# One of four weight sums moved to DRAM, and three more seven-product groups, in a hybrid decoder layer

## The chip, the cores and the metric

One core of a Trainium2 chip runs the whole layer in one launch. The metric is device microseconds of one execution. Engines are named as in the profile: PE is TensorE (PEld its weight loads), DVE is VectorE, ACT is ScalarE, POOL is GpSimd, SP is SyncE; a name with a q (SPq, ACTq) is that engine's queue, which also issues DMAs.

## What is computed

A decoder layer of width 2048 on 256 tokens, float32 throughout:

```python
u = rmsnorm(h, norm_mix_pre)
z, xbc, dt, q, k, v = split(u @ w_in)            # w_in: 2048 x 14368 columns in six parts
y_ssm = ssd(conv_silu(xbc), dt) gated by silu(z) # Mamba-2 scan, 32 heads in 8 groups
y_att = dilated_window_attention(q, k, v)        # 16 heads
h = h + rmsnorm(concat(y_ssm, y_att) @ w_out, norm_mix_post)   # w_out: 4096 x 2048
f = relu(rmsnorm(h, norm_mlp_pre) @ w_up) ** 2                 # w_up: 2048 x 8192
h = h + rmsnorm(f @ w_down, norm_mlp_post)                     # w_down: 8192 x 2048
```

## The kernel before, in words

The weights are 287 MB of traffic and each is used once, on 256 tokens, so the kernel streams weights past activations that stay in SBUF. To reach float32 accuracy, every operand is split into a high part (`hi`, rounded by ACT in `split`, L139) and a remainder (`lo`, subtracted by DVE, L140), and each product becomes three matmuls: high by high, high by low, low by high.

A weight step takes two rows of 128 (KB = 2, one index `k` stands for the pair) by 512 columns (NB): `fetch` loads them as one 512 KB DMA on SP's queue into a tile `raw` (four of them, and in some stages two more in a region called `uc`), and the split fills a pair of tiles `hi` and `lo` (five pairs, BUFS). In the first part (up to about 400 us: SSD projections, queries and keys) features come out on partitions (`gemm_features`, L393 and L396). From the values on, tokens come out on partitions, and a `unit` works on two column blocks at once, for both token tiles.

For each `k` a unit has the choice of two forms. The ordinary one (`row_tiles`, L262 to L264) multiplies two token tiles, two rows and two column blocks directly: 8 products, 24 matmuls. The other one (`seven`, L344 to L346) is a Winograd scheme with seven products, 21 matmuls. For it DVE makes sums of the weights (L225, through `add_in_line`), all of 128x512: with a0, a1 the two rows of the first column block and b0, b1 those of the second, these are a0 + b0, then that + b1, then that + a1, and b0 + b1 in place. The four splits of a seven are those of `raw_a`, of the two-row tile of sums `e`, of `raw_b`, and of one row `t4`. It also needs sums of the activations, made once for a `k` by `sums_of_acts` (L302 to L305 and a split), which a later unit on the same activations uses again. After a unit's last seven, `combine` folds four extra PSUM banks (`more`) into the result. The lists of `k` in each unit, and which of them go by seven, are written out by hand: `V_SEVENS` for the two units of values, `UP_SEVENS` for the seven units of w_up, and literal tuples for two units of w_out, two of the first half of w_down and two of the second. There are 59 sevens. The first unit of w_out begins with `k = 5`; the first five are done before it, between steps of the attention heads.

The order on each engine comes from a scheduler that takes what is ready, by priority, the place in the program being the default priority. Weight work runs in `tc.high_priority(offset=AHEAD)`, that is ahead of all ordinary work. `in_line` keeps the splits and sums of one engine in written order. `tc.issue_after(x)` is the tool for ordering one instruction behind `x`; `attention` (PE behind PE) and `copies` (a DMA of ACT behind an ACT split or, where there is none, behind the last matmul, `product[1]`) use it. Other work is written as generators in a deque, and `pump` runs a step of one of them after each weight step.

POOL does little: zeros at the edge of the convolution (L655), some elementwise steps of the SSD groups (L701, L703, L723), and the powers that make reciprocal roots (L134, L885, L1160). It issues no DMA. `rsqrt_mean` makes `rstd` there, early in the kernel; from it `over_partitions` makes `rbc`, by which the convolutions scale their inputs.

Of the kernel before, what the change touches and what calls it, by code (L numbers as in the profile page):

```python
# [10 lines left out]
F32 = mybir.dt.float32  # L11
# [3 lines left out]
ALU = mybir.AluOpType  # L15

P = 128
# [20 lines left out]
COL_V = COL_K + NH * DH  # L38
NB = 512
KB = 2  # L40
MASKED = -1.0e30
PAIRS = ((128, 1), (512, 4), (2048, 16))
AHEAD = 1_000_000
# [7 lines left out]
FIRST = 3  # L51
UP_SEVENS = (2, 4, 5)
V_SEVENS = (1, 3, 5, 6)


def constants():
# [18 lines left out]
def hymba_layer(ctx: ExitStack, tc: tile.TileContext, x, norm_mix_pre, w_in, conv_w, conv_b, dt_bias, a_log,  # L75
                d_skip, ssm_norm_w, w_out, norm_mix_post, norm_mlp_pre, w_up, w_down, norm_mlp_post,
                consts, out):
    nc = tc.nc
    w_in, w_out, w_up, w_down = w_in[0], w_out[0], w_up[0], w_down[0]
# [61 lines left out]
        return (nc.scalar.activation(hi, src, AF.Copy, scale=scale),  # L141
                nc.vector.scalar_tensor_tensor(lo, src, scale, hi.bitcast(F32), op0=ALU.mult, op1=ALU.subtract))

    def fetch(src, k0, c0, step=KB, into=None):

        raw = wp.tile([P, KB, NB], F32, name="raw", bufs=RAWS) if into is None else into
        for j in range(0, KB, step):
            rs = slice((k0 + j) * P, (k0 + j + step) * P)
            nc.sync.dma_start(raw[:, j:j + step], src[rs, c0:c0 + NB].rearrange("(k p) n -> p k n", p=P))
        return raw  # L150
# [13 lines left out]
    room = {}  # L164
# [22 lines left out]
        room["acts"] = acts  # L187
        sums_of.clear()

    def fetch_next(src, k0, c0):  # L190

        if room["raw"] is None:
            return fetch(src, k0, c0)
        turn = room["turn"]
        room["turn"] += 1
        n = KB * (turn % (RAWS + (NK - SUMS) // KB - 1) - RAWS)
        return fetch(src, k0, c0, into=None if turn < 0 or n < 0 else room["raw"][:, n:n + KB])

    def parts():
        return [wp.tile([P, KB, NB], F32R, name=n, bufs=BUFS) for n in ("hi", "lo")]  # L200
# [2 lines left out]
    product = {}  # L203
# [5 lines left out]
    line = {}  # L209
# [10 lines left out]
        with in_line():  # L220
            line["act"], line["dve"] = split(hi, lo, raw)

    def add_in_line(dst, a, b):
        with in_line():
            line["dve"] = nc.vector.tensor_tensor(dst, a, b, op=ALU.add)  # L225

    def weights(src, k0, c0, fetch=fetch):

# [82 lines left out]
    def seven(src, ca, cb, k, acc, more, first, last):  # L311


        ch, cl = sums_of_acts(k)
        h_, l_, r = room["acts"](k * KB)
        with tc.high_priority(offset=AHEAD):
            raw_a = fetch_next(src, k * KB, ca)
            raw_b = fetch_next(src, k * KB, cb)
            e, t4 = sum_tile(), tmp()
            add_in_line(e[:, 0], raw_a[:, 0], raw_b[:, 0])  # L320
            add_in_line(e[:, 1], e[:, 0], raw_b[:, 1])
            hl_a = parts()
# [12 lines left out]

        def summed(i):
            return ch[:, i], cl[:, i]

        for dst, (a_h, a_l), (hi, lo), j, own in (
                (more[0], block(0, 0), hl_a, 0, True), (acc[0], block(1, 0), hl_a, 1, False),  # L340
                (more[1], summed(1), hl_e, 0, True), (more[2], summed(2), hl_e, 1, True),
                (more[3], summed(0), hl_b, 0, True), (acc[1], summed(3), hl_b, 1, False),
                (acc[2], block(1, 1), hl_t, 0, False)):
            nc.tensor.matmul(dst, a_h, hi[:, j], start=own and first, stop=False)  # L344
            nc.tensor.matmul(dst, a_h, lo[:, j], start=False, stop=False)  # L345
            nc.tensor.matmul(dst, a_l, hi[:, j], start=False, stop=own and last)  # L346
# [12 lines left out]
    def order_of(ks, by_seven):  # L359
        return [(k, k in by_seven) for k in ks]  # L360
# [445 lines left out]
    def keys_too(hb):  # L806
        return queries(COL_Q + hb * NB, rbq), queries(COL_K + hb * NB, rbc)
# [11 lines left out]
    def two_values(vb):  # L819

        if vb:
            room["own"] = deque(mp.tile([P, NT, NB], F32, name="tk", bufs=3)[:, t] for t in range(NT))
        room["sum"] = mp.tile([P, 4, S], F32, name="cT", bufs=5).rearrange("p (k f) s -> p k (f s)", k=KB)
        values = [mp.tile([P, NT, NB], F32, name="tk", bufs=3) for _ in range(2)]
        more = [psmall(), bank(), psmall(), bank()]
        acc = [bank() for _ in range(2 * NT)]

        def end(b):
            def at_end(t, a):
                with tc.high_priority(offset=AHEAD):  # L830
# [5 lines left out]
        unit(w_in[:, COL_V:], vb, order_of(range(7), V_SEVENS), (7,), acc, more,  # L836
             lambda x: combine_new([[v[:, t] for t in range(NT)] for v in values], x), 0, (end(0), end(1)))
        return values

# [236 lines left out]

    in_place_of_u()
    acc = [bank() for _ in range(2 * NT)]
    early = 5
    for k in range(early):  # L1080
# [31 lines left out]
    def whole(n):  # L1112
        def at_end(t, a):
# [18 lines left out]
    def first_hidden(t, acc):  # L1132
# [11 lines left out]
    unit(w_out, 2, order_of((0, 6, 1, 9, 2, 12, 3, 4, 5, 8, 7, 10), (6, 9, 12, 4, 8, 10)), (11, 13, 14, 15), acc, more,  # L1144
         lambda x: combine_new(in_mw(2), x), ending=mix_to_up)
    begun = ended.pop()
    over_partitions(rbc, rmlp)
# [88 lines left out]
    for hf in range(2):  # L1236
        if hf:
            in_place_of_h(act_u)
        for fb in range(0 if hf else 2, 8, 2):
            unit(w_up[:, hf * 4096:], fb, order_of(range(6), UP_SEVENS), (6, 7), acc, more,  # L1240
                 lambda x: combine_new(room["shared"], x), 0, (up_end(fb, 0), up_end(fb + 1, 1)))
            acc, more = more, acc
        if hf == 0:
            in_place_of_h(part)
            unit(w_down, 0, order_of(range(14), (4, 6, 9, 11, 13)), (14, 15), acc, more,
                 lambda x: combine_new(in_mw(0), x), 0, (onto(0), onto(1)))
            unit(w_down, 2, order_of((0, 1, 4, 2, 6, 3, 9, 5, 11, 7, 13, 8), (4, 6, 9, 11, 13)), (10, 12, 14, 15), more, acc,
                 lambda x: combine_new(in_mw(2), x), 0, (onto(2), onto(3)))
    new_h()

# [19 lines left out]
    unit(w_down[4096:], 2, order_of((0, 1, 3, 2, 6, 4, 8, 5, 11, 7, 13, 9), (3, 6, 8, 11, 13, 9)), (10, 12, 14, 15), more, acc,  # L1270
         lambda x: combine_onto(2, x), LAG_DOWN, (complete(2), finish))


# [21 lines left out]
```

## Time and profile before

| | us |
|---|---|
| median of 3 runs | 1473.88 |
| lowest and highest run | 1473.48 and 1474.70 |
| span of the profiled execution, first to last instruction | 1471.1 |
| around the span, by the median | 2.8 |

The profiled execution has no time of its own beside the three runs, so the distance from its span to their median is what stands for the launch around it. A row of the stage table gives a stretch in us, its length, then busy time and number of instructions of each engine, the granted TensorE clock as a share, the mean share of 16 DMA engines, and GB/s. A row of instruction groups gives line, engine, operation, output and inputs with shapes and count, then busy time, mean ns, and the idle time before them with what ended it. A row of waits gives who waited for whom: us in all, times, longest. A row of the timeline gives start and duration in us. A DMA row gives count, size and us from issue to landing.

### The profile page before, as it was taken

Reading aid. Unit: us, or ns where it says so; the run is one execution under the profiler, and the core shown is the slowest. Engines: PE = TensorE matmul, PEld = TensorE weight load, DVE = VectorE, ACT = ScalarE, POOL = GpSimd, SP = SyncE. Lnnn points to the kernel's source line nnn. Section 1 sums busy time; section 2 is a strip of 40 time slices with the busy share of each in tenths; the row PEclk is TensorE's granted clock in tenths of the full one; section 3 lists DMA queues with packets and bytes.
Section 4 is the critical chain, followed back from the end, with each engine's and each line's share of the span. In section 5 each row is a group of like instructions: output and inputs, shape, how many; then the busy total and the mean of one; then the engine's idle time right before and its main releaser. Section 6 shows DMA issues by size and latency. Waiting matters only on the chain.

```text
span 1471.1 us, 20006 instructions
## 1 busy us (share of the span) xinstructions
PE 1461.2 (99%) x7216; PEld 1231.4 (84%) x7216; DVE 1239.6 (84%) x1849; ACT 861.1 (59%) x1188; POOL 47.8 (3%) x67
## 2 busy tenths in 40 slices
PE   9999999999999999999999999999999999999998
PEld 8888888888888888888888888888888888888886
DVE  6798797898497696588989989889887898989998
ACT  7475675465456565555557566655554666665553
POOL 0003100210000000000000000000000000000000
PEclk9999999999999999999999999999999999999999
DMA  7665566555657476566657566655665666576853
GB/s 272 208 205 182 179 184 194 174 172 167 177 168 207 122 208 192 191 229 210 204 177 237 165 194 201 210 175 191 213 223 174 201 201 205 172 235 202 273 200 114
DMA packets 151299, 287.31 MB, mean 195 GB/s; under 512 B 11696, under 2 KB 14624, under 8 KB 151200
## 3 DMA queue, kind: packets, MB, share of 16 engines
q1 hardware_dynamic: 143472, 272.50, 58.9%
q10 hardware_dynamic: 7728, 13.54, 2.8%
q8 instruction: 56, 0.92, 0.3%
q14 instruction: 43, 0.35, 0.1%
HBM read 281.78 MB, written 4.23 MB: 194 GB/s over the span
## 4 chain that ended last, share of the span: by engine, by line
PE 94%; DVE 3%; issue 1%; ACT 1%; DMA 1%; POOL 0%; POOLq 0%; SPq 0%; ACTq 0%; DVEq 0%
PE acc L393 17%; PE acc L262 12%; PE acc L263 12%; PE acc L264 12%; PE acc L396 9%; PE acc L345 4%; PE acc L346 4%; PE acc L344 4%; PE ps L263 3%; PE ps L262 3%; PE ps L264 3%; PE ps L346 2%; PE ps L344 2%; PE ps L345 2%; DVE lo L140 1%
## 5 line engine op out<-in xcount | busy, mean ns | idle before, releaser
L139 ACT ACTIVATE hi<-raw 128x1024 fp32r<-128x1024 f32 (+1 forms) x477 | 499.0, 1053 | 387.9 <-PE acc L393 111.9
L140 DVE TENSOR_TENSOR lo<-raw,hi 128x1024 fp32r<-128x1024 f32 (+1 forms) x477 | 579.9, 1220 | 135.7 <-ACT hi L139 127.9
L393 PE MATMUL acc<-ua,hi 128*128 128x512 f32 x680 | 186.3, 402 | 0.0
L393 PEld LDWEIGHTS acc<-ua,hi 128*128 128x128 f32 x680 | 119.7, 189 | 18.7
L262 PE MATMUL acc<-hi,ua 128*128 128x512 f32 x280 | 112.0, 400 | 0.0
L396 PEld LDWEIGHTS acc<-ua,lo 128*128 128x128 f32 x680 | 99.8, 189 | 11.6
L264 PE MATMUL acc<-hi,ua 128*128 128x512 f32 x280 | 109.3, 391 | 0.0
L263 PE MATMUL acc<-lo,ua 128*128 128x512 f32 x280 | 109.3, 390 | 0.0
L396 PE MATMUL acc<-ua,lo 128*128 128x256 f32 x680 | 102.9, 281 | 0.0
L262 PE MATMUL acc<-hi,sh 128*128 128x512 f32 x224 | 88.7, 397 | 0.0
L264 PE MATMUL acc<-hi,sl 128*128 128x512 f32 x224 | 87.3, 390 | 0.0
L263 PE MATMUL acc<-lo,sh 128*128 128x512 f32 x224 | 87.3, 390 | 0.0
L139 ACT ACTIVATE hi<-e 128x1024 fp32r<-128x1024 f32 x51 | 54.1, 1062 | 55.5 <-DVE e L225 50.3
L393 PE MATMUL acc<-uc,hi 128*128 128x512 f32 x272 | 77.6, 398 | 0.0
L263 PE MATMUL acc<-lo,ah 128*128 128x512 f32 x168 | 65.5, 390 | 0.4 <-DVE lo L140 0.4
L264 PE MATMUL acc<-hi,al 128*128 128x512 f32 x168 | 65.4, 389 | 0.0
L262 PE MATMUL acc<-hi,ah 128*128 128x512 f32 x168 | 65.4, 389 | 0.0
L264 PEld LDWEIGHTS acc<-hi,ua 128*128 128x128 f32 x280 | 52.6, 188 | 11.6
L140 DVE TENSOR_TENSOR lo<-e,hi 128x1024 fp32r<-128x1024 f32 x51 | 62.0, 1216 | 0.0
L262 PEld LDWEIGHTS acc<-hi,ua 128*128 128x128 f32 x280 | 52.6, 188 | 10.4 <-ACT ua L141 0.3
L263 PEld LDWEIGHTS acc<-lo,ua 128*128 128x128 f32 x280 | 52.7, 188 | 10.0
L264 PE MATMUL acc<-hi,uc 128*128 128x512 f32 x144 | 56.0, 389 | 0.0
(475 smaller groups left out, 3060.9 us busy)
## 6 DMA issues: line engine op xcount, KB each, us to landing
raw<-in_w_in_dram SPq DMA_DIRECT2D x189, 512.0 KB, 3.6
raw<-in_w_up_dram SPq DMA_DIRECT2D x128, 512.0 KB, 3.9
raw<-in_w_down_dram SPq DMA_DIRECT2D x110, 512.0 KB, 4.7
raw<-in_w_out_dram SPq DMA_DIRECT2D x46, 512.0 KB, 4.2
uc<-in_w_out_dram SPq DMA_DIRECT2D x18, 512.0 KB, 4.5
uc<-in_w_down_dram SPq DMA_DIRECT2D x18, 512.0 KB, 5.1
bc<-acs_d ACTq DMA_DIRECT2D x8, 512.0 KB, 4.5
xs<-in_x_dram SPq DMA_DIRECT2D x8, 256.0 KB, 6.3
```

Source lines behind the costliest of these rows:

```text
L139: return (nc.scalar.activation(hi, src, AF.Copy), nc.vector.tensor_tensor(lo, src, hi.bitcast(F32), op=ALU.subtract))
L140: nc.vector.tensor_tensor(lo, src, hi.bitcast(F32), op=ALU.subtract))
L262: nc.tensor.matmul(dst, a_h[:, r, ts], hi[:, j], start=begin and j == 0, stop=False)
L263: nc.tensor.matmul(dst, a_h[:, r, ts], lo[:, j], start=False, stop=False)
L264: product[t] = nc.tensor.matmul(dst, a_l[:, r, ts], hi[:, j], start=False, stop=end and j == KB - 1)
L344: nc.tensor.matmul(dst, a_h, hi[:, j], start=own and first, stop=False)
L345: nc.tensor.matmul(dst, a_h, lo[:, j], start=False, stop=False)
L346: nc.tensor.matmul(dst, a_l, hi[:, j], start=False, stop=own and last)
L393: nc.tensor.matmul(acc[f], hi[:, j, f * P:(f + 1) * P], u(k0 + j), start=k0 + j == 0, stop=False, skip_group_check=True)
L396: nc.tensor.matmul(acc[f][:, 0], lo[:, j, f * P:(f + 1) * P], u(k0 + j)[:, 0], start=False, stop=k0 + j == NK - 1, skip_group_check=True)
```

## The change

Two things. First, the sum b0 + b1 is no longer made by DVE. For each seven, POOL's queue issues a copy of b0 (256 KB) from the weights to a fresh DRAM tile `pair<n>`, and then a second DMA that adds b1 to it; `fetch` then loads the row `raw_b[:, 0]` from that tile and `raw_b[:, 1]` from the weights, in two DMAs on SP's queue where it was one. DVE makes three sums instead of four: a0 + (b0 + b1), that - b1, and that + a1. `plan` lists all pairs in the order of use; `next_pair` starts one, and each seven starts the pair of four sevens later (`PAIRS_AHEAD`). The first four are started before the first unit of values.

Second, three more groups go by seven: k = 8 and 10 in w_out's first unit (its order becomes 5, 6, 7, 8, 11, 9, 13, 10, 12), and k = 9 in the first unit of w_down's second half (its order changes too). All three are sevens already in the unit after, on the same activations. There are 62 sevens.

```diff
+PAIRS_AHEAD = 4
...
-    def fetch(src, k0, c0, step=KB, into=None):
+    def fetch(src, k0, c0, step=KB, into=None, pair=None):
         raw = wp.tile([P, KB, NB], F32, name="raw", bufs=RAWS) if into is None else into
+        if pair is not None:
+            nc.sync.dma_start(raw[:, 0], pair)
+            nc.sync.dma_start(raw[:, 1], src[(k0 + 1) * P:(k0 + 2) * P, c0:c0 + NB])
+            return raw
...
+    def plan(name, src, n, order, by_seven):
+        orders[name, n] = order_of(order, by_seven)
+        pairs.extend((src, n * NB, k) for k in order if k in by_seven)
+
+    def next_pair():
+        if not pairs:
+            return
+        src, ca, k = pairs.pop(0)
+        cb = slice(ca + NB, ca + 2 * NB)
+        d = dram.tile([P, NB], F32, name=f"pair{len(paired)}")
+        with ExitStack() as order:
+            for t in product:
+                order.enter_context(tc.issue_after(product[t].ins))
+            nc.gpsimd.dma_start(d, src[k * KB * P:(k * KB + 1) * P, cb])
+        nc.gpsimd.dma_start(d, src[(k * KB + 1) * P:(k * KB + 2) * P, cb], accum_op=ALU.add)
+        paired.append((src, ca, k, d))
+
+    def pair_of(src, ca, k):
+        next_pair()
+        s_, c_, k_, d = paired[turn_of["pair"]]
+        turn_of["pair"] += 1
+        return d
...
             raw_a = fetch_next(src, k * KB, ca)
-            raw_b = fetch_next(src, k * KB, cb)
+            raw_b = fetch_next(src, k * KB, cb, pair_of(src, ca, k))
             e, t4 = sum_tile(), tmp()
-            add_in_line(e[:, 0], raw_a[:, 0], raw_b[:, 0])
-            add_in_line(e[:, 1], e[:, 0], raw_b[:, 1])
+            add_in_line(e[:, 1], raw_a[:, 0], raw_b[:, 0])
+            add_in_line(e[:, 0], e[:, 1], raw_b[:, 1], ALU.subtract)
             hl_a = parts()
             split_in_line(*hl_a, raw_a)
             add_in_line(t4, e[:, 1], raw_a[:, 1])
-            add_in_line(raw_b[:, 0], raw_b[:, 0], raw_b[:, 1])
...
+    plan("out", w_out, 0, (5, 6, 7, 8, 11, 9, 13, 10, 12), (6, 8, 9, 10, 12))
...
+    plan(("down", 1), w_downs[1], 0, (0, 1, 2, 3, 4, 6, 5, 8, 7, 9, 10, 11, 12, 13), (3, 6, 8, 9, 11, 13))
...
     waiting.append(in_place_of_last_heads())
+    for _ in range(PAIRS_AHEAD):
+        next_pair()
     qk.append(keys_too(1))
...
-    unit(w_out, 0, order_of(range(early, 14), (6, 9, 12)), (14, 15), acc, more,
+    unit(w_out, 0, orders["out", 0], (14, 15), acc, more,
          lambda x: combine_new(in_mw(0), x), 0, (whole(0), whole(1)), first=False)
...
-    unit(w_down[4096:], 0, order_of(range(14), (3, 6, 8, 11, 13)), (14, 15), acc, more,
+    unit(w_downs[1], 0, orders[("down", 1), 0], (14, 15), acc, more,
```

More of the change, by code (lines that the diff above doesn't have):

```diff
@@ L40 @@
 KB = 2
+EARLY = 5
 MASKED = -1.0e30
@@ L188, in in_place_of_h, with fetch_next @@
         sums_of.clear()
-    def fetch_next(src, k0, c0):
+    def fetch_next(src, k0, c0, pair=None):
         if room["raw"] is None:
-            return fetch(src, k0, c0)
+            return fetch(src, k0, c0, pair=pair)
         turn = room["turn"]
@@ L196, in fetch_next @@
         n = KB * (turn % (RAWS + (NK - SUMS) // KB - 1) - RAWS)
-        return fetch(src, k0, c0, into=None if turn < 0 or n < 0 else room["raw"][:, n:n + KB])
+        return fetch(src, k0, c0, into=None if turn < 0 or n < 0 else room["raw"][:, n:n + KB], pair=pair)
     def parts():
@@ L357, in combine_new @@
             nc.vector.tensor_tensor(b[1], more[3], b[0], op=ALU.add)
-    def order_of(ks, by_seven):
-        return [(k, k in by_seven) for k in ks]
+    for n in (0, 2):
+        plan("v", w_v, n, range(7), V_SEVENS)
+    plan("out", w_out, 0, (5, 6, 7, 8, 11, 9, 13, 10, 12), (6, 8, 9, 10, 12))
+    plan("out", w_out, 2, (0, 6, 1, 9, 2, 12, 3, 4, 5, 8, 7, 10), (6, 9, 12, 4, 8, 10))
+    for hf in range(2):
+        for n in range(0 if hf else 2, 8, 2):
+            plan(("up", hf), w_ups[hf], n, range(6), UP_SEVENS)
+        if hf == 0:
+            plan(("down", 0), w_down, 0, range(14), (4, 6, 9, 11, 13))
+            plan(("down", 0), w_down, 2, (0, 1, 4, 2, 6, 3, 9, 5, 11, 7, 13, 8), (4, 6, 9, 11, 13))
+    plan(("down", 1), w_downs[1], 0, (0, 1, 2, 3, 4, 6, 5, 8, 7, 9, 10, 11, 12, 13), (3, 6, 8, 9, 11, 13))
+    plan(("down", 1), w_downs[1], 2, (0, 1, 3, 2, 6, 4, 8, 5, 11, 7, 13, 9), (3, 6, 8, 11, 13, 9))
     def unit(src, n, order, last, acc, more, combine, lag=0, at_end=(None, None), first=True, ending=None):
@@ L834, in end @@
             return at_end
-        unit(w_in[:, COL_V:], vb, order_of(range(7), V_SEVENS), (7,), acc, more,
+        unit(w_v, vb, orders["v", vb], (7,), acc, more,
              lambda x: combine_new([[v[:, t] for t in range(NT)] for v in values], x), 0, (end(0), end(1)))
@@ L1078, in hymba_layer @@
     acc = [bank() for _ in range(2 * NT)]
-    early = 5
-    for k in range(early):
+    for k in range(EARLY):
         for b in range(2):
@@ L1142, in first_hidden @@
         split(sh[:, 0:4, ts], sl[:, 0:4, ts], p.rearrange("p (f s) -> p f s", f=4))
-    unit(w_out, 2, order_of((0, 6, 1, 9, 2, 12, 3, 4, 5, 8, 7, 10), (6, 9, 12, 4, 8, 10)), (11, 13, 14, 15), acc, more,
+    unit(w_out, 2, orders["out", 2], (11, 13, 14, 15), acc, more,
          lambda x: combine_new(in_mw(2), x), ending=mix_to_up)
@@ L1239, in hymba_layer @@
         for fb in range(0 if hf else 2, 8, 2):
-            unit(w_up[:, hf * 4096:], fb, order_of(range(6), UP_SEVENS), (6, 7), acc, more,
+            unit(w_ups[hf], fb, orders[("up", hf), fb], (6, 7), acc, more,
                  lambda x: combine_new(room["shared"], x), 0, (up_end(fb, 0), up_end(fb + 1, 1)))
@@ L1244, in hymba_layer @@
             in_place_of_h(part)
-            unit(w_down, 0, order_of(range(14), (4, 6, 9, 11, 13)), (14, 15), acc, more,
+            unit(w_down, 0, orders[("down", 0), 0], (14, 15), acc, more,
                  lambda x: combine_new(in_mw(0), x), 0, (onto(0), onto(1)))
-            unit(w_down, 2, order_of((0, 1, 4, 2, 6, 3, 9, 5, 11, 7, 13, 8), (4, 6, 9, 11, 13)), (10, 12, 14, 15), more, acc,
+            unit(w_down, 2, orders[("down", 0), 2], (10, 12, 14, 15), more, acc,
                  lambda x: combine_new(in_mw(2), x), 0, (onto(2), onto(3)))
@@ L1269, in hymba_layer @@
     waiting.append(copies(of_h, in_dram, 1))
-    unit(w_down[4096:], 2, order_of((0, 1, 3, 2, 6, 4, 8, 5, 11, 7, 13, 9), (3, 6, 8, 11, 13, 9)), (10, 12, 14, 15), more, acc,
+    unit(w_downs[1], 2, orders[("down", 1), 2], (10, 12, 14, 15), more, acc,
          lambda x: combine_onto(2, x), LAG_DOWN, (complete(2), finish))
```

12 lines of the change are left out of this document (10 added, 2 removed).

## The prediction

> **What bounds the kernel now.** I read the page's engine totals first, then the chain that ended last, then TensorE by stage.
>
> ```profile
> span 1471.1 us, 20006 instructions
> PE 1461.2 (99%) x7216; PEld 1231.4 (84%) x7216; DVE 1239.6 (84%) x1849; ACT 861.1 (59%) x1188; POOL 47.8 (3%) x67
> ...
> PEclk9999999999999999999999999999999999999999
> ...
> PE 94%; DVE 3%; issue 1%; ACT 1%; DMA 1%; POOL 0%; POOLq 0%; SPq 0%; ACTq 0%; DVEq 0%
> ```
>
> TensorE is busy 99%, at full granted clock, and holds 94% of the chain. A busy PE need not be a full one, so I take its pace from a stage of pure 512-column products, and then from the two places where seven-product groups run denser than VectorE can feed them:
>
> ```profile
> core 0: us, PE busy (x) PEld busy (x) DVE busy (x) ACT busy (x) POOL busy (x), PEclk, DMA share, GB/s
> 1000.00:1050.00 50.00, 50.00 (x222) 41.40 (x221) 44.30 (x56) 26.61 (x29) 0.00 (x0) 1.00 0.61 200
> 630.00:688.00 58.00, 58.00 (x259) 48.06 (x258) 51.50 (x67) 32.50 (x38) 0.00 (x0) 1.00 0.74 246
> 688.00:750.00 62.00, 62.00 (x275) 51.34 (x274) 59.35 (x78) 38.11 (x44) 0.00 (x0) 1.00 0.59 196
> 430.64:440.74 10.10, 9.84 (x43) 7.78 (x42) 9.85 (x12) 6.93 (x10) 0.00 (x0) 1.00 0.56 163
> 1439.62:1462.13 22.51, 22.10 (x97) 17.94 (x96) 20.26 (x33) 6.93 (x10) 0.54 (x1) 1.00 0.23 79
> ```
>
> In the first row 222 matmuls take 50.00 us: 0.225 us each, and 275 in 62.00 give the same. In the fourth, two sevens in a row (42 matmuls, 9.5 us at that pace) take 10.1: 0.6 us lost. In the last, the four closing blocks (96 matmuls, 21.6 us) take 22.5: 0.9 us lost. The waits of PE and of its weight loads say on what:
>
> ```profile
> PE acc L263 <- DVE lo L140: 0.4, 1, 0.4
> PE acc L345 <- DVE lo L140: 0.3, 1, 0.3
> ```
>
> So VectorE is the second limit, close behind, and whatever is won is won by taking matmuls out or by ending these small waits.
>
> **The change part by part.** *Matmuls.* An ordinary group of one k is 2 column blocks x 2 token tiles x 2 rows x 3 = 24 matmuls; a seven is 7 x 3 = 21. Three groups change: 9 x 0.225 = 2.03 us less TensorE, all of it on the path.
>
> *VectorE.* The rows for its steps, then for the sums of activations that a k needs before its first seven:
>
> ```profile
> L140 DVE TENSOR_TENSOR lo<-raw,hi 128x1024 fp32r<-128x1024 f32 x471 | 575.8, 1227 | 135.5 <-ACT hi L139 127.9
> L139 ACT ACTIVATE hi<-raw 128x1024 fp32r<-128x1024 f32 x471 | 495.3, 1058 | 387.9 <-PE acc L393 111.9 <-PE acc L264 85.9 <-issue 51.9
> L225 DVE TENSOR_TENSOR raw<-raw 128x512 f32<-128x512 f32 x54 | 36.8, 682 | 0.0
> L140 DVE TENSOR_TENSOR lo<-r,hi 128x512 fp32r<-128x512 f32 x51 | 34.9, 683 | 2.7 <-ACT hi L139 2.7
> ...
> L140 DVE TENSOR_TENSOR ua<-r,ua 128x512 fp32r<-128x512 f32 x3 | 2.0, 681 | 0.0
> L302 DVE TENSOR_TENSOR r<-ah,al 128x512 f32<-128x512 f32 x2 | 1.4, 688 | 0.0
> L303 DVE TENSOR_TENSOR r<-r 128x256 f32<-128x256 f32 x3 | 1.3, 417 | 0.0
> L304 DVE TENSOR_TENSOR r<-r 128x128 f32<-128x128 f32 x3 | 0.8, 283 | 0.0
> L305 DVE TENSOR_TENSOR r<-r 128x128 f32<-128x128 f32 x3 | 0.8, 282 | 0.0
> ```
>
> A seven costs VectorE 3 x 1.227 + 0.683 = 4.36 in splits and, before, 4 x 0.682 in sums: 7.09 us. Now it is 3 sums: 6.41. An ordinary group is 2 x 1.227 = 2.45. Over the kernel 59 sevens lose 0.68 each (-40.2) and three groups gain 3.96 each (+11.9): -28 us of a VectorE that mostly isn't the bound. ScalarE splits at most two tiles more in each of the three: 6 x 1.058 = 6.3 us, hidden, since it is busy 59%.
>
> It is not spread evenly. In w_out's first unit (630 to 688) two groups become sevens (+7.9), three sevens lose 0.68 (-2.0), and the sums for k = 8 and 10 move in from the second unit: 0.688 + 0.417 + 0.283 + 0.282 + 0.681 = 2.35 each, +4.7. So 51.5 becomes 62.1, against 58.0 - 1.35 = 56.6 us of TensorE: over by 5.5. Five pairs of split tiles may lie ahead: 5 x 1.227 = 6.1 us of lead, if it is full when the unit begins. Bounds for this term: 0 (lead full, sums made in idle time) to +5.5; nearest is the 0.6 lost in the doubled seven above, and I take +0.5. The second unit gets 59.35 - 4.7 - 4.1 = 50.6 of 62 and runs free. In w_down's second half k = 9 needs its sums one unit earlier, also free.
>
> *Waits that go.* The 0.6 at 430 us and the 0.9 at 1440 sit where sevens crowd, and each seven is 0.68 lighter. Bounds 0 to 1.5; I take 0.9.
>
> *The pair in DRAM.* The rows for its DMAs: stores to and loads from a DRAM tile of the same 256 KB, SP's cost of one issue, and the stream beside which they run:
>
> ```profile
> h_d<-ha ACTq DMA_DIRECT2D x6, 256.0 KB, 4.3
> ha<-h_d ACTq DMA_DIRECT2D x6, 256.0 KB, 6.9
> ...
> q1 hardware_dynamic: 143472, 272.50, 58.9%
> ...
> L149 SPq DMA_DIRECT2D raw<-in_w_in_dram x15: 367/368/368, 407.2 to 444.5; - x15
> ```
>
> SP issues one DMA more for each of 62 sevens: 62 x 0.368 = 23 us of a queue with nothing else, hidden. It now also waits for the adding transfer; behind that wait stand the next raw tiles. Pool issues a copy, waits for it, and issues the addition: 8.6 to 13.8 us a pair by the two rows, none of it shown for Pool's own queue. The pair is started four sevens ahead: at least 30 us in the densest unit (six sevens in 62 us), so it lands early, and 62 x 13.8 = 856 us fits into the time after Pool's last head work. Queue q1 needs 0.589 x 1471 / 272.5 = 3.18 us of all 16 engines per MB; a pair is 0.52 MB written, and 0.79 if the addition's second read counts: 1.7 to 2.5 us, 103 to 155 in all, or 7 to 11% on a share near 0.6. The first slice of the kernel lives at 0.80, so I take 0 here; the range is 0 to the rival below.
>
> Sum: -2.03 + 0.5 - 0.9 = -2.4 us. The span would be 1468.7; the runs' median lies 2.8 us above the span, which I carry over: **1471.5 us**. The ends give 1470.0 (no cost, both waits gone) to 1477; I let this case's own range end at 1473. About 0.2%, 2.95 us, is what a measurement tells from no change: the forecast is inside it.
>
> **The rivals.** *1. Pool's list comes too early.* The copy reads an input and writes a fresh DRAM tile, so it waits for nothing. What becomes of such work in this program's queues?
>
> ```profile
> 38.45 0.70 POOL L134 TENSOR_TENSOR rstd<-rm,half 128x2 f32<-128x2 f32 x1 [2.45 <-DVE rm L133]
> L553 DVE COPY rbc<-ps x1: 417/417/417, 57.0 to 57.0; 128x256 f32<-128x256 f32 x1
> ...
> 178.58 0.33 ACTq L678 DMA_DIRECT2D bc<-acs_d  x1
> L710 DVE TENSOR_SCALAR bc<-bc,acs x16: 275/279/281, 185.7 to 208.7; 128x128 f32<-128x128 f32 x16
> 260.54 0.66 POOL L701 TENSOR_TENSOR xdd<-xdt,toend 128x256 f32<-128x256 f32 x1 [15.18 <-DVE xdt L699]
> ...
> 788.35 0.33 ACTq L1190 DMA_DIRECT2D h_d<-hb  x1
> 797.36 0.39 PE L264 MATMUL acc<-hi,uc 128*128 128x512 f32 x1
> ```
>
> The load of bc for the fifth SSD group is issued at 178.6, when its buffer comes free, 82 us before that group's own xdd; work is put where its inputs allow, not where it is written. The issue_after around the new copy names matmuls. The one place before with that form is L1190: its last DMAs stand behind product[1], the matmul at 797.4, and one goes out at 788.35, so a matmul didn't hold another engine's queue. And most pairs are made under AHEAD, over Pool's ordinary work. Then the list of 124 DMAs stands at Pool's head, and rstd (38.45 now, needed for rbc at 57.0) behind it. Price: at 0.33 us an issue the list takes 41 us and rstd is still in time; at the engines' 103 to 155 us rbc is 46 to 98 us late; one DMA after another would be far more. The stream meanwhile wants a 0.6 share; if the two queues share evenly it gets 0.5, and a stage stretches by 0.6 / 0.5. I price the case at about +50 less 2: 1522, and 1476 to 1572 with its bounds. It decides once Pool's list runs past 55 us. Against it: no row shows work pulled forward by more than 82 us, nor over an engine's own earlier work, and four pairs are placed at the heads on purpose.
> The Trainium skill, "DMA: Bandwidth & Descriptors", section "Issuing engines are not separate DMA queues", says that DMAs run on the same 16 engines and interleave whoever issues them; no run here shows Pool's, but it speaks for the stretch. By the same page's section "Anatomy of one DMA", a 256 KB transfer from Pool would take an estimated 2.0 + 0.6 = 2.6 us, a pair 5.2, under the rows' 8.6.
>
> *2. VectorE bounds w_out's first unit.* The full 5.5 us is lost there: -2.0 + 5.5 - 0.4 = +3.1, 1477. For it: the sums of groups 8 and 10 wait for two tiles of r. Against: DVE is idle 6.5 us of that window now, being ahead. It decides if the lead at 630 us is under two pairs.
>
> *3. Pairs land late.* SP stands at a pair and the raws behind it. With six sevens in 62 us Pool has 10.3 us a pair; at 13.8 it falls behind by 3.5 us each, 21 in the unit, unless it ran ahead before. Price to +10: 1481. Against: nothing but Pool's own few instructions (its 47.8 us) keeps it from running ahead. The Trainium skill, "SBUF — State Buffer", section "SBUF: two separate sides", says that Pool can't write its descriptors while VectorE holds their shared port in a 2-port mode. VectorE's work in the sevens takes two inputs, which by that page isn't such a mode against a descriptor write; no row shows it, and it leaves rival 3 its small chance.
>
> *4. The change doesn't do what it says:* the nine matmuls are counted from the program and can't come back, so I give it no chance of its own.
>
> **How the numbers follow.** Forecast case 0.50, of which about 0.24 clears 2.95 us (waits gone, no new one) and 0.26 not; rival 1: 0.36; rival 2: 0.08; rival 3: 0.06. Rivals 1 and 3 and most of 2 are slower by over 0.2%: faster 0.24, same 0.26, slower 0.50. Signs are split, so beside the forecast's 1470.0 to 1473.0 the range must reach into rival 1: 1470.0 to 1535.0 leaves out some 0.05 below and 0.15 above.
>
> **What would show it.** In the profile after: matmul count down by 9; L225 with three rows a seven (no raw<-raw), DVE near 1211 us; Pool's DMAs starting after 340 us for the forecast, at the span's start with rstd far behind 38 us for rival 1; windows of w_out's first unit at 56.6 us, or up to 62 for rival 2; SP waiting on the pair's landing for rival 3. A time over 1477 makes the forecast wrong, and one under 1470 says that more waits hung on the fourth sum than these rows show.

## The result, and the profile after

| | before | after |
|---|---|---|
| median, us | 1473.68 | 1574.66 |
| lowest and highest of four runs | 1473.48 and 1474.70 | 1573.99 and 1576.65 |
| ratio, with its 95% interval | | 1.0686 (1.0671 to 1.0700) |

The change costs 101 us. The page of the kernel after, engine totals and slices:

```profile
span 1572.2 us, 20288 instructions
PE 1475.5 (94%) x7207; PEld 1240.1 (79%) x7207; DVE 1216.3 (77%) x1805; ACT 870.3 (55%) x1194; POOL 127.3 (8%) x191
PE   6858099999999999999999999999999999999998
...
PEclk9779599999999999999999999999999999999999
DMA  9999986566655664765676566665657566676763
```

Nine matmuls are gone, as the change says, and VectorE has 23 us less to do. From the sixth slice on (about 200 us) TensorE is as full as before. Ahead of that it isn't, and there the 16 DMA engines are at 90% or more. The stages, in the columns of the prediction's stage table:

```profile
0.00:50.00 50.00, 33.16 (x165) 28.42 (x166) 17.36 (x30) 19.83 (x39) 18.82 (x32) 0.90 1.02 276
50.00:100.00 50.00, 28.07 (x135) 23.72 (x134) 14.69 (x21) 15.01 (x25) 21.75 (x32) 0.74 1.01 269
100.00:150.00 50.00, 47.24 (x251) 40.74 (x250) 18.81 (x22) 14.98 (x21) 16.45 (x25) 0.99 1.05 297
150.00:200.00 50.00, 8.87 (x31) 6.95 (x30) 8.88 (x13) 6.93 (x7) 21.82 (x32) 0.56 0.97 233
533.75:543.27 9.52, 9.52 (x43) 7.88 (x42) 8.88 (x11) 7.64 (x9) 0.00 (x0) 1.00 0.68 175
1541.42:1563.18 21.76, 21.76 (x97) 18.02 (x96) 18.61 (x32) 6.17 (x9) 0.54 (x1) 1.00 0.19 68
```

In the first 200 us TensorE is busy 117 us. GpSimd's timeline and its DMA rows show what runs there:

```profile
1.26 2.32 POOL L256 DMA_DIRECT2D pair<-in_w_in_dram  x4 [0.81 <-POOLq L1338]
5.98 0.88 POOL L257 DMA_DIRECT2D pair<-in_w_in_dram  x1 [2.40 <-DMA pair<-in_w_in_dram]
...
192.73 0.76 POOL L136 TENSOR_TENSOR rstd<-rm,half 128x2 f32<-128x2 f32 x1
...
210.40 3.35 POOL L257 DMA_DIRECT2D pair<-in_w_in_dram  x4 [6.90 <-DMA pair<-in_w_in_dram]
...
439.32 0.70 POOL L136 TENSOR_TENSOR gr<-rm,half 128x2 f32<-128x2 f32 x1 [3.99 <-DVE rm L135]
1559.51 0.54 POOL L1215 TENSOR_TENSOR rff<-mean,half 128x1 f32<-128x1 f32 x1 [652.18 <-DVE mean L1214]
```

```profile
pair<-in_w_down_dram POOLq DMA_DIRECT2D x44, 256.0 KB, 8.1
pair<-in_w_up_dram POOLq DMA_DIRECT2D x42, 256.0 KB, 9.6
```

The pairs are made from 1.26 us on, in rounds of four copies, a wait and four additions, and rstd (38.45 us before) stands behind 114 of the 124 DMAs until 192.73 us. TensorE's waits, and those of the engines that feed it:

```profile
ACT hi L141 <- DMA raw<-in_w_in_dram: 79.7, 38, 9.9
PE ps L606 <- DVE dg L605: 41.1, 1, 41.1
DVE dg L605 <- POOL rstd L136: 33.8, 1, 33.8
PE ps L634 <- DVE wdt L142: 16.3, 1, 16.3
```

So there are two kinds of loss in the same 200 us. The weight stream's loads come late: a 512 KB load of w_in issued in the first 100 us lands in 12.1 us (median) where it took 4.4, and ScalarE waits 79.7 us for w_in's tiles, 69.8 of them in the first 200 us (the 16.3 us at wdt is such a load too). And one wait of 41.1 us hangs on rstd, through dg. Two events that both kernels have, the last gr of the SSD and the first rff, tell how much is lost where. Before:

```profile
336.21 0.70 POOL L134 TENSOR_TENSOR gr<-rm,half 128x2 f32<-128x2 f32 x1 [3.99 <-DVE rm L133]
...
1458.45 0.54 POOL L1160 TENSOR_TENSOR rff<-mean,half 128x1 f32<-128x1 f32 x1 [654.22 <-DVE mean L1159]
```

The gr is 103.1 us later (439.32 - 336.21), the rff 101.1 (1559.51 - 1458.45). Everything is lost ahead of 440 us, and the part of the kernel that the change was about is 2.05 us shorter than it was.

### The profile page after: what moved, and what is told of

Same layout as the page of the kernel before. It is cut to its first block, busy times and chain, and to the rows that moved or that the text cites. A ratio compares the mean times of both kernels' runs of the same rounds, so it can differ in the third digit from the quotient of the medians.

```text
span 1572.2 us, 20288 instructions
## 1 busy us (share of the span) xinstructions
PE 1475.5 (94%) x7207; PEld 1240.1 (79%) x7207; DVE 1216.3 (77%) x1805; ACT 870.3 (55%) x1194; POOL 127.3 (8%) x191
## 4 chain that ended last, share of the span: by engine, by line
PE 79%; issue 8%; DMA 5%; DVE 5%; POOL 2%; ACT 0%; POOLq 0%; DVEq 0%; ACTq 0%
PE acc L447 12%; PE acc L309 10%; PE acc L307 10%; PE acc L308 10%; PE acc L450 6%; PE acc L388 4%; PE acc L390 4%; PE acc L389 4%; PE ps L307 3%; PE ps L309 3%; PE ps L308 3%; DVE lo L142 2%; PE ps L390 2%; PE ps L389 2%; PE ps L388 2%
## 5 line engine op out<-in xcount | busy, mean ns | idle before, releaser
L447 PE MATMUL acc<-ua,hi 128*128 128x512 f32 x680 | 190.6, 408 | 12.8 <-ACT hi L141 5.6
L141 ACT ACTIVATE hi<-e 128x1024 fp32r<-128x1024 f32 x54 | 57.3, 1062 | 59.9 <-DVE e L231 50.3
L142 DVE TENSOR_TENSOR lo<-e,hi 128x1024 fp32r<-128x1024 f32 x54 | 65.8, 1218 | 0.0
L309 PE MATMUL acc<-hi,al 128*128 128x512 f32 x148 | 57.6, 389 | 0.0
L308 PE MATMUL acc<-lo,ah 128*128 128x512 f32 x148 | 57.6, 389 | 0.0
L307 PE MATMUL acc<-hi,ah 128*128 128x512 f32 x148 | 57.1, 389 | 0.0
```

Source lines behind the costliest of these rows:

```text
L141: return (nc.scalar.activation(hi, src, AF.Copy), nc.vector.tensor_tensor(lo, src, hi.bitcast(F32), op=ALU.subtract))
L142: nc.vector.tensor_tensor(lo, src, hi.bitcast(F32), op=ALU.subtract))
L307: nc.tensor.matmul(dst, a_h[:, r, ts], hi[:, j], start=begin and j == 0, stop=False)
L308: nc.tensor.matmul(dst, a_h[:, r, ts], lo[:, j], start=False, stop=False)
L309: product[t] = nc.tensor.matmul(dst, a_l[:, r, ts], hi[:, j], start=False, stop=end and j == KB - 1)
L447: nc.tensor.matmul(acc[f], hi[:, j, f * P:(f + 1) * P], u(k0 + j), start=k0 + j == 0, stop=False, skip_group_check=True)
```

## The experiments

Theory A: the whole loss is the copies' time. They wait for nothing, so they run at the start, and there they cost twice: they crowd the weight stream (crowding), and they stand in front of GpSimd's own work (the hold on rstd). Rivals: the transfers cost wherever they lie (B); VectorE in w_out's first unit (C); GpSimd's queue alone (D); later, GpSimd's late reads in the paced kernels (F). Times of kernels with an interval are medians; the others are one execution.

| kernel | us | before, same chip | ratio, 95% |
|---|---|---|---|
| list | 1591.35 | 1472.87 | |
| list_small | 1512.30 | 1472.87 | |
| hold | 1597.90 | 1472.87 | 1.0839 (1.0823 to 1.0855) |
| hold2 | 1510.57 | 1473.72 | |
| ordinary | 1577.78 | 1474.13 | |
| paced | 1480.24 | 1472.87 | 1.0055 (1.0039 to 1.0071) |
| paced2 | 1491.85 | 1473.72 | 1.0118 (1.0091 to 1.0144) |
| paced2_59 | 1485.70 | 1473.72 | 1.0087 (1.0067 to 1.0107) |
| paced59 | 1476.07 | 1473.40 | 1.0019 (1.0010 to 1.0028) |
| spread | 1493.59 | 1473.40 | 1.0139 (1.0122 to 1.0157) |
| dve62 | 1478.35 | 1473.72 | 1.0031 (1.0019 to 1.0042) |
| few | 1477.33 | 1473.40 | 1.0028 (1.0017 to 1.0038) |

**list: the transfers alone.** On the kernel before:

```diff
+    with tc.high_priority(offset=AHEAD):
+        for i, (src, n, k) in enumerate(...):          # the 62 of the change
+            d = dram.tile([P, NB], F32, name=f"pair{i}")
+            nc.gpsimd.dma_start(d, src[k * KB * P:(k * KB + 1) * P, cb])
+            nc.gpsimd.dma_start(d, src[(k * KB + 1) * P:(k * KB + 2) * P, cb], accum_op=ALU.add)
```

> The kernel before, with its own 59 sevens and four sums on VectorE, and only the 124 GpSimd transfers of the change added at the start, over the stream; nobody reads what they make. Theory A: the transfers alone carry the whole loss, 1570 to 1582 us (1574.7 and 9 matmuls, 2 us, more). Rival B (the loss lies with the sevens that wait for the loads of pair): 1474 to 1490 us.

1591.35 us, 118 over the kernel before. GpSimd's timeline, then the waits:

```profile
212.22 1.74 POOL L134 TENSOR_TENSOR rstd<-rm,half 128x2 f32<-128x2 f32 x1
```

```profile
ACT hi L139 <- DMA raw<-in_w_in_dram: 93.1, 39, 10.1
PE ps L571 <- DVE dg L570: 47.5, 1, 47.5
```

The same two waits, both larger. The transfers carry the whole loss, and nothing that the sevens do with them is needed for it. It is 9 us more than the range expected, in one execution. Part of that lies in the list itself: here rstd stands behind 122 of the 124 DMAs, after the change behind 114, because there the first four pairs come last, at 201 us. A round of four pairs takes 11 to 14 us in the changed kernel, and rstd is 19.5 us later here.

**list_small: the same issues without the data.** As list, with copies of 8 columns, 4 KB.

> As the run with the list alone, but with 8 columns of each copy instead of 512: 4 KB for 256 KB, the same 124 issues on GpSimd. What is left is GpSimd's queue. By the issues' rows (0.6 us a copy, 0.83 us an addition, some 2 us until four have landed) four pairs take about 8 us, the list 120 us, and rstd comes at about 120 to 125 us where the stream, undisturbed, has about 100 us of work ahead of the place where it needs rstd: theory A in two parts gives 15 to 30 us of loss, 1490 to 1505 us. If GpSimd's queue is the whole of it (rival D): 1560 to 1576 us. If transfers are the whole: 1473 to 1476 us.

1512.30 us, 39 over. GpSimd's timeline, the wait, and the issues:

```profile
101.78 2.42 POOL L134 TENSOR_TENSOR rstd<-rm,half 128x2 f32<-128x2 f32 x1
```

```profile
PE ps L571 <- DVE dg L570: 32.8, 1, 32.8
```

```profile
pair<-in_w_up_dram POOLq DMA_DIRECT2D x42, 4.0 KB, 3.6
```

With next to nothing to move, 122 of the 124 DMAs still keep rstd until 101.78 us, and the wait behind rstd is 32.8 us. So the hold on rstd costs up to 39 us by itself; the small transfers aren't quite nothing, since w_in's 512 KB loads of the first 100 us land in 5.7 us for 4.4. The expectation put rstd 20 us later and the loss at 15 to 30 us: TensorE had some 70 us of work ahead of that place (it stood 32.8 us until shortly behind rstd), not the 100 that the changed kernel's trace suggested.

**hold and hold2: the copies behind the SSD.** On the changed kernel, the copies are ordered behind the latest pow of rsqrt_mean, an instruction of GpSimd's own queue. In hold2 the first four are made with high priority too.

```diff
-            for t in product:
-                order.enter_context(tc.issue_after(product[t].ins))
+            for t in last_pool:                        # the latest pow of rsqrt_mean
+                order.enter_context(tc.issue_after(t.ins))
...
+    with tc.high_priority(offset=AHEAD):               # hold2 only
         for _ in range(PAIRS_AHEAD):
             next_pair()
```

> The changed kernel with all copies ordered behind the latest pow of the SSD on GpSimd's queue: none starts before about 336 us, then all 62 in a burst, some 14 us for four, so to about 550 us. Theory A in two parts, transfers that crowd the weight stream and GpSimd's queue that holds rstd: here the second part is gone (rstd at 38 us) and the first is moved to 336 to 550 us, where the stream needs 0.6 of the transfer engines: 1485 to 1530 us, likeliest 1500. Rival D (GpSimd's queue alone makes the loss): about 1472 us. Rival B (transfers cost wherever they lie): 1500 to 1574.

1597.90 us, 125 over, and none of the expected ways. The waits of hold and one stage:

```profile
DVE cT L233 <- DMA raw<-pair: 123.9, 3, 121.7
```

```profile
450.00:500.00 50.00, 0.00 (x0) 0.00 (x0) 0.00 (x0) 0.00 (x0) 26.40 (x40) 0.50 0.86 190
```

The first seven waits 121.7 us for its pair. The four first pairs are made outside the high-priority block, so they stand last in a list of 62: a pair late after all, rival 3's mechanism, but by the order of the list. The changed kernel has the same order (its last four additions, at 210.40 us, are w_in's), only long before anyone reads them. hold2 takes that away:

> As the hold run, whose loss was one wait of 123 us for the first pair, because the four first pairs stood last on GpSimd's queue; here they stand first. What is left is the crowding of the weight stream alone, from 336 us on, without GpSimd's hold on rstd: by the changed kernel's 100 to 150 us (PE busy 47.24 us of 50 at a share of 1.05) it is 3 to 6 us for 50 us, over some 200 us, so 12 to 24 us, less 2 for the matmuls, and 4 to 6 for w_out: 1483 to 1500 us. If crowding is the larger half of the 101 us: 1510 to 1540 us. If GpSimd's queue is all of it: 1476 to 1479 us.

1510.57 us, 37 over, at the edge of the expectation's second branch. The stages of hold2 from the first copies on:

```profile
340.00:390.00 50.00, 46.45 (x270) 40.71 (x269) 31.93 (x47) 22.29 (x32) 18.93 (x30) 0.99 1.05 305
390.00:440.00 50.00, 47.37 (x214) 39.00 (x215) 28.65 (x35) 19.25 (x23) 20.81 (x31) 0.91 1.01 271
440.00:490.00 50.00, 34.92 (x138) 28.03 (x137) 30.45 (x49) 22.66 (x31) 16.33 (x24) 0.81 1.03 279
```

GpSimd holds no other work back here, rstd is early, and TensorE still stands idle 21 us of 150 while the share is over 1. So crowding alone costs 37 us at this place. Each half costs 37 to 39 us alone and both together 101; they do not simply add up. The traces offer two reasons, neither tried by itself: crowding makes the list longer (rstd at 192.73 us against 101.78), and the start of the kernel needs a larger share than the place of hold2. Before, the first stage and the first of those above:

```profile
0.00:50.00 50.00, 48.79 (x288) 43.45 (x289) 32.56 (x52) 33.64 (x62) 1.11 (x7) 1.00 0.80 268
...
340.00:390.00 50.00, 50.00 (x290) 43.93 (x289) 35.80 (x50) 25.59 (x34) 0.00 (x0) 1.00 0.64 186
```

It is 0.80 there and 0.64 here.

**ordinary: priority instead of order.** The pairs' calls moved out of the high-priority block.

```diff
+        pair = pair_of(src, ca, k)
         with tc.high_priority(offset=AHEAD):
             raw_a = fetch_next(src, k * KB, ca)
-            raw_b = fetch_next(src, k * KB, cb, pair_of(src, ca, k))
+            raw_b = fetch_next(src, k * KB, cb, pair)
```

> The changed kernel, with its copies and additions made at ordinary priority instead of ahead of all ordinary work (one line moved out of the high-priority block); nothing orders them behind the sevens. GpSimd's queue then has 45 of the 124 DMAs before the first pad and rstd, the rest between the convolutions' pads, all before the SSD's own steps. By the changed kernel's 14 us for eight DMAs, rstd comes at about 75 to 85 us instead of 192.73, ahead of the 100 us of work that the stream has; the crowding at the start stays. If GpSimd's hold on rstd and crowding add up, the 41 us gap at rstd goes and the stream's own loss of about 50 to 60 us stays, with new waits for pads: 1525 to 1545 us. If crowding is all, 1570; if the pads, each behind up to 12 DMAs (some 20 us), take over as the wait: 1550 to 1575 us.

1577.78 us. GpSimd's timeline and TensorE's waits:

```profile
85.37 1.03 POOL L136 TENSOR_TENSOR rstd<-rm,half 128x2 f32<-128x2 f32 x1
```

```profile
PE ps L770 <- POOL xdd L756: 23.8, 1, 23.8
PE ps L635 <- DVE wdt L142: 20.8, 1, 20.8
```

rstd is there at 85 us, as expected, and the loss stays the same. TensorE no longer waits for it, but 23.8 us for xdd, a later step of GpSimd that stands behind the pads and the rest of the list, and 20.8 us for wdt, a late load. That is nearest the third branch of the expectation, 3 us above its range. Which of GpSimd's steps is waited for changes with the order of the list; the list is there in both.

**paced: what the change says it does.** A one-element multiply on GpSimd reads the split of a seven, and the next copy is ordered behind it.

```diff
             split_in_line(*hl_b, raw_b)
+            last_pool[:] = [nc.gpsimd.tensor_tensor(half[:, 15:16], hl_b[0][:, 0, 0:1].bitcast(F32),
+                                                    half[:, 0:1], op=ALU.mult)]
+            next_pair()                                # no longer in pair_of
```

> The changed kernel, with the copies truly paced: a one-element multiply on GpSimd reads the split of a seven, and the next copy is ordered behind it on GpSimd's own queue; the first four copies are ordered behind the last pow of the SSD (336 us in the kernel before). Same 124 transfers, same three more sevens. Theory A (the loss is only the copies' time: all of them at the start, over the weight stream and in front of GpSimd's rstd): rstd back at 38 us, stages to 400 us as before, DMA share 0.60 to 0.75 after that, whole run 1471.5 us (1470 to 1474). Rival B (the transfers cost wherever they lie: the loads of pair arrive late, or the stream is stretched by 2 us a pair): 1480 to 1560. Rival C (VectorE's list in w_out's first unit sets the end): 1474 to 1478, with a loss of 3 to 6 us between 700 and 800 us.

1480.24 us (1476.72 to 1485.60): 94 us of the 101 are back. The same transfers, moved in time, cost little, and that settles the main cause. But theory A's 1470 to 1474 is missed: the time lies at the lower edge of B's range and 2 us above C's. What is left was tried in parts.

**dve62: the three more sevens without DRAM.** All four sums on VectorE, as before the change.

```diff
-            raw_b = fetch_next(src, k * KB, cb, pair_of(src, ca, k))
+            raw_b = fetch_next(src, k * KB, cb)
...
+            add_in_line(raw_b[:, 0], raw_b[:, 0], raw_b[:, 1])
```

> The three more sevens alone: all four sums on VectorE as before, no transfer through DRAM. Theory C with its own sum: VectorE gets five sums of 0.68 us more in w_out's first unit than in the paced run, so the gap there grows from 6.0 to about 9 us: 1478 to 1484 us. If VectorE has room there: 9 matmuls less, 1470 to 1472 us.

1478.35 us, as C expected. The stage of w_out's first unit in dve62, then in paced:

```profile
632.00:700.00 68.00, 64.10 (x278) 51.35 (x277) 67.17 (x94) 38.85 (x50) 0.00 (x0) 1.00 0.67 221
```

```profile
632.00:700.00 68.00, 64.19 (x275) 50.30 (x274) 63.02 (x87) 38.88 (x50) 25.00 (x16) 1.00 0.84 254
```

In dve62 VectorE is busy 67.17 us of 68 there, and TensorE stands idle 3.9: theory C. In paced VectorE has 4 us less to do, and TensorE stands as long (3.8). There the trace shows another wait, for the one-element multiply that paces the copies:

```profile
ACT hi L143 <- POOL half L375: 5.6, 3, 2.7
...
645.01 10.15 POOL L375 TENSOR_TENSOR half<-hi,half 128x1 f32<-128x1 f32 x1 [2.53 <-ACT hi L143]
```

The multiply reads a hi tile, and ScalarE can't fill that tile again before it is done. At 645.01 us it takes 10.15 us (its median in paced is 0.65), and ScalarE waits 5.6 us for it and two others; for a load of w_out's tiles it doesn't wait at all in this stage. So part of paced's 7.4 us comes from the pacing, and theory F has something to it; how much was not tried apart.

**paced2 and paced2_59.** Each addition goes behind the next seven's multiply, so that GpSimd doesn't wait for a copy while it holds a hi tile; paced2_59 has the 59 sevens of before.

```diff
+            whole_pairs()                              # the addition to the pair of the seven before
             next_pair()                                # the copy alone
```

> As the first paced run, but each addition into DRAM stands behind the next seven's one-element multiply on GpSimd's queue, so GpSimd no longer waits 5 to 8 us for a copy to land while a hi tile is held for it. The first paced run was 7.4 us over the kernel before, with 6.0 us of matmul gaps between 650 and 700 us, in w_out's first unit. Theory F (GpSimd's late reads of hi made the stalls): 1471 to 1473 us and no gap over 1 us between 650 and 700. Theory C (VectorE's list in w_out's first unit, two more sevens): the gap stays, 1476 to 1479 us.

> As that, with the 59 sevens and the orders of the kernel before: 118 transfers, one sum less on VectorE in every seven, no more sevens, so as many matmuls as before. If spread transfers cost nothing and the stalls of the paced run came with the added sevens (theory C): 1472 to 1474 us, within 0.1% of the kernel before. If the transfers or the ticks cost by themselves (theories B, F): 1475 to 1480 us.

1491.85 and 1485.70 us, both above their expectations; paced2 is worse than paced, and paced2_59 worse than paced59 (below). The later additions did not help, and with 59 sevens there is a loss that C doesn't cover. They don't clear F either: paced2 has a multiply of 10.15 us in the same unit (at 652.19 us). And they changed a second thing: each pair is whole one seven later, and VectorE's waits for pairs grow from 6.0 us to 11.6 (62 sevens) and 17.0 (59).

**paced59 and spread.** paced with the 59 sevens; and that with the pairs made but not read, four sums on VectorE as before.

```diff
-    plan("out", w_out, 0, (5, 6, 7, 8, 11, 9, 13, 10, 12), (6, 8, 9, 10, 12))
+    plan("out", w_out, 0, range(5, 14), (6, 9, 12))
...
-            raw_b = fetch_next(src, k * KB, cb, pair_of(src, ca, k))    # spread only
+            raw_b = fetch_next(src, k * KB, cb)
```

> As the first paced run (addition right behind its copy), with the 59 sevens and orders of the kernel before. If that run's 7.4 us are VectorE's in w_out's first unit: 1472.5 to 1475 us (the 2.6 us of gaps that it had elsewhere, less what one sum less frees). If the copies' crowding of single loads is as large as in the run with the later additions: 1479 to 1486 us.

> As that, but nobody reads the pairs: the sevens load both blocks and take four sums on VectorE as before, so the spread transfers and the ticks are all that is added to the kernel before. If loads of the stream that meet a copy land late, that alone costs: 1475 to 1486 us. If the loss of the paced runs is the wait for pairs (raw<-pair, 5.8 to 17 us of waits there): 1473 to 1475 us.

1476.07 and 1493.59 us: the first 1 us above its lower branch, the second 8 above its upper one. The load of w_up's tiles and ScalarE's wait for it, before and in spread:

```profile
raw<-in_w_up_dram SPq DMA_DIRECT2D x128, 512.0 KB, 3.9
...
ACT hi L139 <- DMA raw<-in_w_up_dram: 23.9, 23, 1.6
```

```profile
raw<-in_w_up_dram SPq DMA_DIRECT2D x128, 512.0 KB, 4.5
...
ACT hi L143 <- DMA raw<-in_w_up_dram: 37.7, 25, 4.4
```

59 spread pairs that nobody reads, with the multiplies that pace them, cost 20 us: the median load takes 4.5 us for 3.9, and the longest wait for one 4.4 for 1.6. Reading them, which takes a sum of 0.68 us from each seven and splits one load of each in two, gives 17.5 of it back (1493.59 - 1476.07). But the loads are no earlier in paced59:

```profile
raw<-in_w_up_dram SPq DMA_DIRECT2D x107, 512.0 KB, 4.6
...
ACT hi L143 <- DMA raw<-in_w_up_dram: 35.1, 25, 5.2
```

So late loads alone don't make the 20 us. They cost it where VectorE has the fourth sum to make as well (busy 1240.5 us in spread, 1206.6 in paced59); how the two act together isn't shown. So the sum that VectorE no longer makes is worth about as much as the transfers that make it elsewhere cost, and the balance of the exchange, without the added sevens, is +2.7 us (1.5 to 4.1).

**few: pairs only where VectorE is short.** Eleven pairs, for w_out's first unit and the first unit of w_down's second half, made hundreds of us ahead.

```diff
+            made = ca == 0 and (src is w_out or src is w_downs[1])
+            raw_b = fetch_next(src, k * KB, cb, pair_of(src, ca, k) if made else None)
```

> The 62 sevens, with sums through DRAM in only two units: the five sevens of w_out's first unit and the six of w_down's last first unit, the two that hold the three more; the other 51 take all four sums on VectorE as before. Eleven pairs, one behind each seven of w_v and three in w_up, hundreds of us before they are read. If the spread copies cost by number (2.6 to 12 us for 59 to 62), eleven cost 0.5 to 2 us; VectorE's gap in w_out's first unit falls from 5.1 us (three more sevens alone) to the 1.6 us of the run hold2: 9 matmuls less (-2.0), +1.6, +0.5 to +2: 1473 to 1476 us. If copies that are few and early cost nothing: 1471.5 to 1473 us.

1477.33 us, above both expectations. In w_out's first unit TensorE gets most of what it lost in dve62 back:

```profile
632.00:700.00 68.00, 66.62 (x294) 54.41 (x293) 65.76 (x91) 39.76 (x51) 0.00 (x0) 1.00 0.66 223
```

It loses elsewhere: from 400 to 500 us, where its first copies run, TensorE is busy 97.28 us, before 99.73 and in dve62 100.00. No kernel tried is faster than the one before.

## Why the prediction was wrong

Point by point, in its own order.

*Matmuls, -2.03.* Right: 7216 to 7207.

*VectorE, 1211 us after.* 1216.3, 5 us off.

*Waits that go, -0.9.* Right in kind, small in size. The two sevens in a row take 9.52 us for 10.10 and the four closing blocks 21.76 for 22.51 (the last two stage rows of after): -1.33, and both stages now run at 0.227 us a matmul (9.52 / 42, 21.76 / 96).

*w_out's first unit, +0.5.* Too small by 0.9 where the pairs were there long before, since TensorE's timeline after has one wait of 1.4 us in it:

```profile
775.89 0.50 PE L388 MATMUL acc<-hi,ua 128*128 128x512 f32 x1 [1.38 <-ACT hi L141]
```

With copies beside it or with four sums it stands 3.8 to 3.9 us. The bound of 5.5 was the better guide, and "nearest is the 0.6 lost in the doubled seven" was not a reason.

*Sum past the heads: -2.4.* Measured -2.05, from the last gr to rff. The forecast is the right price of a change whose pairs cost nothing. Two small slips: with its own terms the lower end is 1470.4, not 1470.0 (1473.88 - 2.03 - 1.5), and the 2.8 us around the span is about 1 too much, since the runs with a span on record lie 1.7 to 1.9 us above it, before and after.

*The pair in DRAM, 0.* This is the step that failed, in three places. "The pair is started four sevens ahead" was read from the program; nothing of before's trace supported it, and rival 1's own rows (L1190's DMA at 788.35 us ahead of the matmul at 797.36 that it names) spoke against it. The copies went out from 1.26 us on, and their list cost 101 us. Behind an instruction of GpSimd's own queue the same call did hold: in hold2 the first copies go out at 339.20 us, behind the gr of 338.56. Second, "so it lands early ... I take 0": even paced, 59 pairs cost 20 us if nothing is won by them (spread, multiplies included). The share of 7 to 11% was right in size (in hold, with the stream standing, 20 pairs in 50 us at 0.86 are 2.15 us of all engines each, inside the 1.7 to 2.5), but a mean share says nothing of a load that meets a copy. Third, once the copies were there, one sum less in each seven gave 17.5 us back (paced59 against spread), and the sum had no term for that: its 0.9 is for a kernel without copies.

*Rival 1, 0.36 and 1522.* This is what happened, mechanism and marks: the copies at the span's start, rstd late, the stream stretched. Its price of 50 us was half of the 101, and its bound of 1572 was passed too. "At 0.33 us an issue the list takes 41 us and rstd is still in time" took SP's price for GpSimd's queue: in a run of four, a copy takes 0.58 us of GpSimd's time (2.32 / 4) and an addition 0.84 (3.35 / 4), and with the waits between them 122 DMAs with 4 KB each hold rstd until 101.78 us. The list of the changed kernel, 190 us, is longer than the 155 of the upper bound: each round of four pairs also waits until its copies have landed, 6.90 us at 210.40. And the two losses were priced as if one hid the other. The Trainium skill, "DMA: Bandwidth & Descriptors", section "Issuing engines are not separate DMA queues", says that DMAs of all issuers share 16 engines and interleave. The trace agrees: a share of 1.02, and SP's loads land in 12.1 us for 4.4 beside GpSimd's transfers. By that rule crowding needed a price of its own, and hold2 shows it: 37 us.

*Rival 2, 0.08.* Not the cause here, but real: TensorE stands idle 3.9 us of w_out's first unit in dve62, and the whole kernel is 4.6 us slower. *Rival 3, 0.06.* Large only in hold (121.7 us); in the paced kernels VectorE waits 6 to 17 us for pairs in all.

What stays open: how the 7.4 us of paced divide among late loads, late pairs, the multiplies that pace the copies and VectorE's list; and by which way the missing sum gives 17.5 us back. Most of SP's waits end with VectorE's split, so earlier splits may let loads start earlier; that was not tried.

## What to carry to other kernels

The transfers of this change depended on nothing and ran at once: ask of each new queue entry what it waits for, on its own queue, and what stands behind it. Moving work from a nearly full engine to the DMAs of a kernel that streams at a share of 0.6 was here an exchange and no gain: price the single load that meets the copy, not the mean share. And when a trace already shows rows against a forecast's premise, that rival is the forecast. Last, what paces a transfer is work too, and it can hold a buffer.

## What the runs showed of the hardware

A DMA issued by GpSimd is work for GpSimd: the 124 of the change raise its busy time from 47.8 to 127.3 us, 0.64 us each, where SP's issue takes 0.37. The Trainium skill, "DMA: Bandwidth & Descriptors", section "Anatomy of one DMA — SWDGE (gpsimd) path", calls the making of descriptors small and says that many descriptors can be emitted before its cost shows. The rows don't show descriptors apart; the DMAs as a whole did show, since with 4 KB each 122 of them still kept rstd until 101.78 us, their waits for landing included. By its formula 256 KB take an estimated 2.6 us; the rows have 8.1 to 9.6 us beside the stream.

A small operation of GpSimd can last as long as VectorE doesn't pause. Paced's multiply of 10.15 us ends at 655.16 us; VectorE runs operations with two inputs without a gap from 643.80 on and first pauses at 655.11. All ten multiplies of over 2 us in paced, paced2, paced59 end 0.04 or 0.05 us after VectorE's first pause since their start, a pause of 0.03 us being enough. Two of the four in spread don't end at a pause, so this isn't the only way, and it was not tried by itself.

A wait costs more than its length. TensorE's granted clock is 0.50 in a long one (hold, 450 to 500 us), and the first matmuls behind the 16.3 us wait of the changed kernel go at about half their pace: the granted clock is 0.50 from 96.30 to 100.00 us, where the same matmuls before had 1.00 (48.90 to 50.50 us). Over the kernel TensorE is busy 14.3 us longer than before (1475.5 for 1461.2), with nine matmuls fewer. After, then before, the same instruction:

```profile
96.28 0.47 PE L634 MATMUL ps<-ua,wdt 128*64 128x256 f32 x1 [16.30 <-DVE wdt L142]
96.55 0.41 PE L635 MATMUL ps<-ua,wdt 128*64 128x256 f32 x1
96.77 0.41 PE L634 MATMUL ps<-ua,wdt 128*64 128x256 f32 x1
```

```profile
48.94 0.28 PE L580 MATMUL ps<-ua,wdt 128*64 128x256 f32 x1
49.06 0.28 PE L581 MATMUL ps<-ua,wdt 128*64 128x256 f32 x1
```

One starts every 0.22 us where it was every 0.12.
